# Hybrid streaming encoder on one core: Down's loads and splits issued from a table of steps, and the first FFN unit's token operands made product by product

## The chip, the cores and the metric

The kernel runs on one of the eight cores of a Trainium2 chip. The metric is device time in microseconds (us) of one execution; smaller is better. A core has five engines with queues of their own: PE (TensorE, matrix products), DVE (VectorE), ACT (ScalarE), POOL (GpSimd) and SP, which in this kernel issues nearly all DMA transfers. Each engine runs its queue strictly in order, and semaphores make an instruction wait for another engine or for a transfer.

## The reference

One layer with 1024 prompt tokens and 32 sample tokens (T = 1056), D_MODEL = 1024, D_FF = 2816, all in float32. The change lies in the second half, the ConvFFN:

```python
    x = x + jnp.einsum('ble,ed->bld', jnp.concatenate([y_a, y_b, y_c], axis=-1), w_out)

    h2 = _rmsnorm(x, norm_ffn_g)
    up, gate = jnp.split(jnp.einsum('bld,df->blf', h2, w_up), 2, axis=-1)
    g_conv, new_f = _causal_dwconv(gate, st_f, conv_ffn_w)
    x = x + jnp.einsum('blf,fd->bld', jax.nn.silu(g_conv) * up, w_down)
    return x, (new_a, new_ssm, new_b, new_c, new_f)
```

A final RMSNorm over x gives `y_prompt` and `y_sample`. The mixers ahead of it (short gated conv, Mamba-2 scan, Conformer conv) are not touched.

## The kernel before

**Products in float32 parts.** PE multiplies in the type fp32r. Each operand is split: ACT copies it to fp32r (hi), DVE subtracts that from the original (lo). A product is hi*hi + hi*lo + lo*hi, three matmuls into one PSUM bank. So every operand costs an ACT copy and a DVE subtraction of its size before PE can use it.

**Out-projection, second part (o2).** Its eight products end the first half. After each chunk of tokens (`CH`: 256, 384, 416 columns) `e_o2` writes the new residual row block, adds its square into `ss2`, and scales a copy into `rows[m]`. With the last block (m = 7) `rms_factor` turns `ss2` into `rf`, the reciprocal root, chunk by chunk: a matmul with ones on PE, Sqrt on ACT, RECIPROCAL on DVE (L1007).

**Up.** For each of NF = 22 column blocks f of 128 a `Unit` computes up and gate together by seven Strassen products P1 to P7 over half-sized operands (24 matmuls of 264 columns each). Token operands `X[i, k]` (tiles named XP...: 7 products x 4) are the same for every unit; they are made from `rows` before the first unit: `make_x` forms sums and differences (`xt`), `split_x` the two parts (L1143 on ACT, L1144 on DVE). Weight operands come per unit from `make_sums` (L1162 to L1165) and `make_w` (L1175, L1176), three products ahead. `after` evacuates PSUM: P1's bank is copied to `s1` by ACT (L1292), and P2 accumulates on the same bank, so P2 waits for that copy. `finish` does the causal conv, silu and product, and stores `u` to DRAM (`midd[f]`, L1327).

**Down.** Two passes h over 512 output columns each. In a pass, three groups take the token chunks in the order `CORDER[h]`; in a group PE runs over f: 4 output tiles x 3 matmuls of the chunk's width. Each f needs a weight row block (`next_wd`: load 256 KB, split; kept for the pass) and a token row block (`next_mid`: load, split). Both are iterators, one f per call, called in the loop right ahead of PE's matmuls:

```python
                for f in range(NF):
                    if h == 0 and (n != 1 or f > 14):
                        next_wd()
                    next_mid()
```

Token rows land in `small("midr")`, a ring of 4 buffers; weights land in the pool of 44 shared slots. At f = 21 of Up `next_wd` is called twice and, from the fourth product, `next_mid` twice per product, as a head start. `final` and `final_half` are the closing norms, per chunk, in pass 1.

**What sets the order.** The code is recorded in program order; a scheduler then orders each engine's queue by priority, which is mostly that order, and places waits where a slot is taken over from an earlier user.

Of the kernel before, what the change touches and what calls it, by code (L numbers as in the profile page):

```python
# [9 lines left out]
F32 = mybir.dt.float32  # L10
F32R = mybir.dt.float32r
ALU = mybir.AluOpType
# [4 lines left out]
P = 128  # L17
# [66 lines left out]
def hybrid_stream_encoder_step(  # L84
# [10 lines left out]
    with ctx:  # L95
# [1090 lines left out]
        for m in range(8):  # L1186
# [5 lines left out]
            def e_o2(j, c0, w, ps, m=m, r=r, x=x):  # L1192
# [11 lines left out]
                if j == 2:  # L1204
# [3 lines left out]
                    if m == 6:  # L1208
                        make_w(0, "P1")
                        make_w(0, "P2")  # L1210
                if m == 7:
                    rms_factor(rf, ss2, c0, w, "misc")
                if j == 2:
                    split_x("P2" if m > 3 else "P1", m % 4, x[:, 0:H])

# [2 lines left out]
        for fn in deferred:  # L1218
            fn()
        deferred.clear()  # L1220
        del ss2, rb
        psum.close()
        banks = tc.tile_pool(name="banks", bufs=8, space=PSUM, reuse_waits="tile")
        psum = ExitStack()
# [8 lines left out]
        C2 = [(0, H // 2), (H // 2, H // 2)]  # L1233
        ORDER = ("P1", "P5", "P6", "P2", "P7", "P3", "P4")
        fpack = const.tile([P, 2, 2, NF], F32, name="fpack")
        midd = [dram.tile([P, T], F32, name=f"mid{f}") for f in range(NF)]
        def make_x(i, k):

            a, b = rows[k], rows[k + 4]
# [15 lines left out]
        class Unit:  # L1255
# [62 lines left out]
            def finish(self):  # L1318
                f, gb, u = self.f, self.gb, self.u
                take_state(fpack, gb, 2, f)  # L1320
                ca = slot(T + 2, name="ca")
                for _ in conv_steps(ca, 2, lambda i: pcol(at["w_f"] + NF * i + f), whole(gb, 2)):
                    pass
                act.activation(ca, ca, AF.Silu)
                for t, a, n in run_pieces(2):
                    v.tensor_tensor(out=u[:, t:t + n], in0=ca[:, a:a + n], in1=u[:, t:t + n], op=ALU.mult)
                dma(out=midd[f], in_=u)  # L1327


        wd, mids = {}, {}  # L1330
        w_jobs = iter([(h, f) for h in range(2) for f in range(NF)])
        CORDER = ((0, 1, 2), (2, 1, 0))
        m_jobs = iter([(h, j, f) for h in range(2) for j in CORDER[h] for f in range(NF)])

        def next_wd():
            for h, f in w_jobs:
                r = slot(512, name="rawd")
                dma(out=r, in_=w_down[0, f * P:(f + 1) * P, 512 * h:512 * h + 512])
                w = wd[h, f] = slot(1024, F32R, name="wd")
                act.activation(w[:, 0:512], r, AF.Copy)  # L1340
                v.tensor_tensor(out=w[:, 512:1024], in0=r, in1=w[:, 0:512].bitcast(F32), op=ALU.subtract)
                return

        def next_mid():
            for h, j, f in m_jobs:
                c0, w = CH[j]
                r = small("midr")
                dma(out=r[:, 0:w], in_=midd[f][:, c0:c0 + w])
                q = slot(832, F32R, name="mhl")
                a, b = q[:, 0:416], q[:, 416:832]  # L1350
                act.activation(a[:, 0:w], r[:, 0:w], AF.Copy)  # L1351
                v.tensor_tensor(out=b[:, 0:w], in0=r[:, 0:w], in1=a[:, 0:w].bitcast(F32), op=ALU.subtract)  # L1352
                mids[h, j, f] = (a, b)
                return

        FIRST_ORDER = ("P1", "P2", "P5", "P6", "P3", "P7", "P4")
        for i in FIRST_ORDER[2:]:
            if i == "P5":
                make_sums(0)
            for k in range(4):  # L1360
                make_x(i, k)
            make_w(0, i)
            if i == "P6":
                load_up(1)
        rows.clear()
        xt_.clear()
        steps = [(f, i) for f in range(NF) for i in (ORDER if f else FIRST_ORDER)]
        AHEADW = 3
        for n, (f, i) in enumerate(steps):
            last = f == NF - 1  # L1370
            if n % 7 == 0:
# [3 lines left out]
                make_sums(f + 1)  # L1375
            if 7 <= n + AHEADW < len(steps):
                make_w(*steps[n + AHEADW])
            unit.product(i)
            if n % 7 == 4:
                raws.pop(f)  # L1380
# [2 lines left out]
            if last:  # L1383
                for k in range(4):
                    X.pop((i, k))
                next_wd()
                next_wd()
                if n % 7 > 2:
                    next_mid()
                    next_mid()  # L1390
        del unit, rf
        scope.close()
        scope = ExitStack()

# [65 lines left out]
        for h in range(2):  # L1460
# [4 lines left out]
            for n, j in enumerate(CORDER[h]):  # L1465
# [1 line left out]
                if h and j == 0:  # L1467
                    final_half(0)
                ps = [bank() for _ in range(4)]
                for f in range(NF):  # L1470
                    if h == 0 and (n != 1 or f > 14):
                        next_wd()
                    next_mid()
                    if n == 0 and f in (8, 10, 12, 14):
                        load_res(4 * h + f // 2 - 4)
                    q = wd[h, f]
                    a, b = mids.pop((h, j, f))
                    for m in range(4):
                        o = ps[m][:, 0:w]
                        hi, lo = q[:, m * P:m * P + P], q[:, 512 + m * P:512 + m * P + P]  # L1480
                        pe.matmul(o, hi, a[:, 0:w], start=(f == 0), stop=False)  # L1481
                        pe.matmul(o, hi, b[:, 0:w], start=False, stop=False)  # L1482
                        pe.matmul(o, lo, a[:, 0:w], start=False, stop=(f == NF - 1))  # L1483
                    if n == 2:
                        del wd[h, f], q
                for m in range(4):
                    rc = res[4 * h + m][:, c0:c0 + w]
                    v.tensor_tensor(out=rc, in0=rc, in1=ps[m][:, 0:w], op=ALU.add)
# [35 lines left out]
```

## Time and profile before

| | |
|---|---|
| Time, median of 3 runs | 1572.89 us (1572.78 to 1575.14) |
| The profiled execution's own time | 1571.52 us |
| Its span in the trace | 1569.2 us |
| PE busy | 1497.7 us (95%) |
| DVE busy | 1082.8 us (69%) |
| ACT busy | 606.3 us (39%) |
| Mean granted TensorE clock | 0.983 of full speed |

The time of an execution is 2.3 us more than its span. Busy time is summed over stages with different limits: PE's 95% says that gaps are few, not where they are, and its matmuls are pipelined with modelled ends, so a busy PE can still run at half its clock. What a stage could give back is read from the stage: from the start of its first matmul to that of the next stage's, against the number of matmuls in it and the distance of two matmuls that wait for nothing.

### The profile page before, as it was taken

How to read it: one execution, taken by the hardware profiler on the slowest of the kernel's cores; microseconds unless marked ns; L12 is line 12 of the kernel's file. 1: busy time of each engine (PE TensorE's matmuls, PEld its weight loads, DVE VectorE, ACT ScalarE, POOL GpSimd, SP SyncE). 2: the span in 40 equal slices, each digit the busy share in tenths (PEclk: the TensorE clock that was granted, in tenths of full speed). 3: DMA queues.
4: the chain of work that ended last, by engine and by line, in shares of the span. 5: the costliest groups of instructions: out<-in, count | busy, mean ns of one | idle time of the engine just before them, and what ended most of it. 6: DMA issues, size and time to landing. Idle time of an engine off the chain costs nothing.

```text
span 1569.2 us, 25496 instructions
## 1 busy us (share of the span) xinstructions
PE 1497.7 (95%) x10205; PEld 1455.0 (93%) x10205; DVE 1082.8 (69%) x1677; ACT 606.3 (39%) x1156; POOL 92.2 (6%) x213
## 2 busy tenths in 40 slices
PE   7999999999999899999779999999999977989998
PEld 7999999999989789999779999999999866979998
DVE  7467979598587489675788888888888743343323
ACT  6411112534665374343353333444333333242322
POOL 1000100011121121000020000000000000000000
PEclk9999999999999899999989999999999998999999
DMA  5513011311353586553203322222222256355312
GB/s 189 188 34 102 16 55 45 78 41 41 92 131 97 128 243 165 174 170 126 69 28 89 89 82 82 82 82 82 69 69 69 89 160 201 113 162 176 108 62 101
DMA packets 184420, 163.92 MB, mean 104 GB/s; under 512 B 12117, under 2 KB 165103, under 8 KB 184303
## 3 DMA queue, kind: packets, MB, share of 16 engines
q1 hardware_dynamic: 184287, 162.30, 35.0%
q8 instruction: 80, 1.31, 0.3%
q14 instruction: 37, 0.30, 0.1%
q10 hardware_dynamic: 16, 0.00, 0.0%
HBM read 125.19 MB, written 37.08 MB: 103 GB/s over the span
## 4 chain that ended last, share of the span: by engine, by line
PE 88%; DMA 5%; DVE 4%; ACT 2%; issue 1%; SPq 0%; POOL 0%; ACTq 0%; DVEq 0%; POOLq 0%
PE g L228 14%; PE g L233 14%; PE g L232 13%; PE g L1278 9%; PE g L1280 9%; PE g L1279 9%; PE g L1481 4%; PE g L1482 4%; PE g L1483 4%; DMA rawd<-in_w_down_dram 4%; PE yd L876 1%; PE st L866 1%; PE yo L871 1%; DVE XP L1144 1%; DMA yar<-yad 0%
## 5 line engine op out<-in xcount | busy, mean ns | idle before, releaser
L1278 PE MATMUL g<-XP,wop 128*128 128x264 f32 x1232 | 354.5, 288 | 13.2 <-ACT ps L1292 9.0
L1280 PE MATMUL g<-XP,wop 128*128 128x264 f32 x1232 | 351.7, 286 | 1.4 <-DVE wop L1176 1.4
L1279 PE MATMUL g<-XP,wop 128*128 128x264 f32 x1232 | 352.1, 286 | 0.0
L228 PE MATMUL g<-hH,hi 128*128 128x416 f32 (+2 forms) x952 | 309.7, 325 | 0.0
L232 PE MATMUL g<-hL,hi 128*128 128x416 f32 (+2 forms) x952 | 307.3, 323 | 0.0
L233 PE MATMUL g<-hH,lo 128*128 128x416 f32 (+2 forms) x952 | 307.3, 323 | 0.0
L1278 PEld LDWEIGHTS g<-XP,wop 128*128 128x128 f32 x1232 | 235.3, 191 | 17.9 <-ACT ps L1292 9.2
L1280 PEld LDWEIGHTS g<-XP,wop 128*128 128x128 f32 x1232 | 234.2, 190 | 1.7 <-DVE wop L1176 1.6
L1279 PEld LDWEIGHTS g<-XP,wop 128*128 128x128 f32 x1232 | 234.6, 190 | 0.4 <-issue 0.4
L1481 PE MATMUL g<-mhl,wd 128*128 128x256 f32 (+2 forms) x528 | 159.3, 333 | 26.9 <-ACT mhl L1351 25.3
L228 PEld LDWEIGHTS g<-hH,hi 128*128 128x128 f32 x952 | 179.8, 189 | 1.8 <-issue 1.2
L232 PEld LDWEIGHTS g<-hL,hi 128*128 128x128 f32 x952 | 179.8, 189 | 0.4
L233 PEld LDWEIGHTS g<-hH,lo 128*128 128x128 f32 x952 | 179.6, 189 | 0.5 <-DVE lo L183 0.2
L1482 PE MATMUL g<-mhl,wd 128*128 128x256 f32 (+2 forms) x528 | 175.0, 335 | 2.4 <-DVE mhl L1352 2.2
L1483 PE MATMUL g<-mhl,wd 128*128 128x256 f32 (+2 forms) x528 | 171.5, 328 | 0.0
L273 DVE SCALAR_TENSOR_TENSOR cacc<-cb,par,cacc 128x1086 f32<-128x1086 f32 (+1 forms) x120 | 159.2, 1327 | 7.3 <-ACT cacc L270 5.7
L1352 DVE TENSOR_TENSOR mhl<-midr,mhl 128x256 fp32r<-128x256 f32 (+2 forms) x132 | 67.2, 521 | 89.0 <-ACT mhl L1351 88.5
L1481 PEld LDWEIGHTS g<-mhl,wd 128*128 128x128 f32 x528 | 96.6, 193 | 32.2 <-ACT mhl L1351 29.7
L1482 PEld LDWEIGHTS g<-mhl,wd 128*128 128x128 f32 x528 | 103.0, 195 | 6.9 <-DVE mhl L1352 5.7
L1483 PEld LDWEIGHTS g<-mhl,wd 128*128 128x128 f32 x528 | 103.2, 196 | 0.6
L1351 ACT ACTIVATE mhl<-midr 128x256 fp32r<-128x256 f32 (+2 forms) x132 | 64.0, 493 | 99.6 <-PE g L1483 75.8
L268 ACT ACTIVATE ca<-gb,par 128x1058 f32<-128x1058 f32 x22 | 26.0, 1181 | 185.7 <-issue 159.0
(315 smaller groups left out, 2438.5 us busy)
## 6 DMA issues: line engine op xcount, KB each, us to landing
rawf<-in_w_up_dram SPq DMA_DIRECT2D x44, 512.0 KB
raw<-in_w_in_dram SPq DMA_DIRECT2D x40, 512.0 KB
mid<-u SPq DMA_DIRECT2D x22, 528.0 KB
rawd<-in_w_down_dram SPq DMA_DIRECT2D x44, 256.0 KB
midr<-mid SPq DMA_DIRECT2D x44, 208.0 KB
midr<-mid SPq DMA_DIRECT2D x44, 192.0 KB
E<-acd SPq DMA_DIRECT2D x16, 512.0 KB
midr<-mid SPq DMA_DIRECT2D x44, 128.0 KB
```

The lines of the kernel that those rows point to most:

```text
L228: pe.matmul(o, hi[:, k, :], x, start=first, stop=False)
L232: pe.matmul(o, hi[:, k, :], y, start=False, stop=False)
L233: pe.matmul(o, lo[:, k, :], x, start=False, stop=last)
L273: v.scalar_tensor_tensor(out=out[:, u:u + n], in0=buf[:, b + j:b + j + n], scalar=w_of(j), in1=out[:, u:u + n], op0=ALU.mult, op1=ALU.add)
L1278: pe.matmul(o, hi, xh, start=(new and k == 0), stop=False, **kw)
L1279: pe.matmul(o, hi, xl, start=False, stop=False, **kw)
L1280: pe.matmul(o, lo, xh, start=False, stop=(k == 3), **kw)
L1351: act.activation(a[:, 0:w], r[:, 0:w], AF.Copy)
L1352: v.tensor_tensor(out=b[:, 0:w], in0=r[:, 0:w], in1=a[:, 0:w].bitcast(F32), op=ALU.subtract)
L1481: pe.matmul(o, hi, a[:, 0:w], start=(f == 0), stop=False)
L1482: pe.matmul(o, hi, b[:, 0:w], start=False, stop=False)
L1483: pe.matmul(o, lo, a[:, 0:w], start=False, stop=(f == NF - 1))
```

## The change

**Down.** The two iterators go. A table made beforehand gives each of the 66 steps (a pair of rows f, f + 1 in one group; q counts pairs, NPAIR = 11) the loads and the splits to be issued at it. Loads are of two rows at a time: `[128, 2, 512]` weights, `[128, 2, w]` tokens, for which `midd` becomes 11 DRAM tiles of two rows. Landing tiles all come from the 44 shared slots (`rawd`), token parts too. Token rows are loaded 4 steps and split 2 steps before their use, weights loaded 6 and split 3 steps before in pass 0, and from step 16 on for pass 1. The seven products of the last unit count as steps -7 to -1. Pass 0 takes its chunks widest first, (2, 1, 0) instead of (0, 1, 2).

**First unit.** The token operands of P5, P6, P3, P7 and P4 are no longer all recorded ahead of the unit: `first(i)` is called in the loop, P5's before product 0 (P1), P6's before product 1, and so on (`FIRST_AHEAD`). `rms_factor` for `rf` moves from the end of o2 to behind P4's operands.

```diff
-                if m == 7:
-                    rms_factor(rf, ss2, c0, w, "misc")
...
-        midd = [dram.tile([P, T], F32, name=f"mid{f}") for f in range(NF)]
+        midd = [dram.tile([P, 2, T], F32, name=f"mid{f}") for f in range(NF // 2)]
...
-                dma(out=midd[f], in_=u)
+                dma(out=midd[f // 2][:, f % 2, :], in_=u)
+        NPAIR = NF // 2
+        CORDER = ((2, 1, 0), (2, 1, 0))
+        loads, splits = {}, {}
+        for h in range(2):
+            for q in range(NPAIR):
+                at0 = 3 * NPAIR * h + q
+                c = at0 - 3 if h == 0 else min(at0 - 12, 2 * NPAIR + q - 3)
+                splits.setdefault(c, []).append(("w", h, q))
+                loads.setdefault(c - 3, []).append(("w", h, q))
+            for n, j in enumerate(CORDER[h]):
+                for q in range(NPAIR):
+                    at0 = 3 * NPAIR * h + NPAIR * n + q
+                    splits.setdefault(at0 - 2, []).append(("m", h, q, j))
+                    loads.setdefault(at0 - 4, []).append(("m", h, q, j))
+        rawd, wd, mids = {}, {}, {}
+
+        def prepare(step):
+
+            for job in loads.pop(step, ()):
+                h, q = job[1:3]
+                r = rawd[job] = slot(1024, name="rawd")
+                if job[0] == "w":
+                    src = w_down[0, 2 * q * P:2 * q * P + 2 * P, 512 * h:512 * h + 512]
+                    dma(out=r.rearrange("p (a m) -> p a m", a=2), in_=src.rearrange("(a p) m -> p a m", p=P))
+                else:
+                    c0, w = CH[job[3]]
+                    dma(out=r[:, 0:2 * w].rearrange("p (a w) -> p a w", a=2), in_=midd[q][:, :, c0:c0 + w])
+            for job in splits.pop(step, ()):
+                h, q = job[1:3]
+                r = rawd.pop(job)
+                if job[0] == "w":
+                    for a in range(2):
+                        w = wd[h, 2 * q + a] = slot(1024, F32R, name="wd")
+                        src = r[:, 512 * a:512 * a + 512]
+                        act.activation(w[:, 0:512], src, AF.Copy)
+                        v.tensor_tensor(out=w[:, 512:1024], in0=src, in1=w[:, 0:512].bitcast(F32),
+                                        op=ALU.subtract)
+                else:
+                    w = 2 * CH[job[3]][1]
+                    if w <= 512:
+                        t = slot(1024, F32R, name="mhl")
+                        hi, lo = t[:, 0:w], t[:, 512:512 + w]
+                    else:
+                        hi, lo = slot(w, F32R, name="mh"), slot(w, F32R, name="ml")
+                    act.activation(hi, r[:, 0:w], AF.Copy)
+                    v.tensor_tensor(out=lo, in0=r[:, 0:w], in1=hi.bitcast(F32), op=ALU.subtract)
+                    mids[job[1:]] = (hi, lo)
...
+            if i == "P4":
+                for c0, w in CH:
+                    rms_factor(rf, ss2, c0, w, "misc")
...
+        FIRST_AHEAD = [("P5",), ("P6",), ("P3",), ("P7",), ("P4",), (), ()]
...
+            if f == 0:
+                for i2 in FIRST_AHEAD[n]:
+                    first(i2)
...
-                next_wd()
-                next_wd()
-                if n % 7 > 2:
-                    next_mid()
-                    next_mid()
+                prepare(n % 7 - 7)
...
+                for q in range(NPAIR):
+                    prepare(3 * NPAIR * h + NPAIR * n + q)
```

**Where instructions move: SP's queue at the start of Down.** `rawd<-in_w_down_dram` is a load of weights, `midr<-mid` (before) or `rawd<-mid` (changed) one of token rows, `mid<-u` a unit's store, `res` a residual row. Before, one weight row and one token row in turn:

```order
L1327 DMA mid_7365<-u 128x1056
L1348 DMA midr<-mid_7354 128x256
L1348 DMA midr<-mid_7355 128x256
L1338 DMA rawd<-in_w_down_dram 128x512
L1348 DMA midr<-mid_7356 128x256
L1338 DMA rawd<-in_w_down_dram 128x512
L1348 DMA midr<-mid_7357 128x256
```

Changed, pairs. The rows shown are the last ones ahead of the last unit's store (`mid_7342<-u`):

```order
L1325 DMA mid_7342<-u 128x1056
L1352 DMA rawd<-in_w_down_dram 128x2x512
L1355 DMA rawd<-mid_7332 128x2x416
L1352 DMA rawd<-in_w_down_dram 128x2x512
L1355 DMA rawd<-mid_7333 128x2x416
L1352 DMA rawd<-in_w_down_dram 128x2x512
L1355 DMA rawd<-mid_7334 128x2x416
L474 DMA out_dram<-st_o 44x128 x2
L1352 DMA rawd<-in_w_down_dram 128x2x512
L1355 DMA rawd<-mid_7335 128x2x416
L1352 DMA rawd<-in_w_down_dram 128x2x512
L1355 DMA rawd<-mid_7336 128x2x416
```

Six weight pairs (the first above the rows shown) and five token pairs stand ahead of that store; the sixth token pair and the seventh weight pair stand behind it. There are half as many issues, each of two rows, and no longer one row each of both kinds in turn.

**ACT's queue in the first unit.** The copies L1143 and L1175 are the hi parts (XP50 is P5's first token operand, XP60 P6's, XP30 P3's, XP40 P4's); L1292 (L1290 in the changed kernel) is the copy of P1's bank that P2 waits for. Before, that copy stands behind the hi parts of all operands:

```order
L1143 ACTIVATE XP40_7460<-xt34_7433 128x528
L1143 ACTIVATE XP41_7463<-xt34_7439 128x528
L1143 ACTIVATE XP42_7466<-xt34_7445 128x528
L1143 ACTIVATE XP43_7469<-xt34_7451 128x528
L1175 ACTIVATE wop_7472<-rawf_6890 128x512
L1292 ACTIVATE ps15_7477<-g_7481 128x264
L1292 ACTIVATE ps15_7477<-g_7495 128x264
```

Changed, it stands behind P5's alone; and P5's own copies (`g_7476`, `g_7491`) now stand ahead of P3's operands:

```order
L1143 ACTIVATE XP53_7376<-xt12_7373 128x528
L1175 ACTIVATE wop_7379<-s12_7349 128x512
L1290 ACTIVATE ps15_7345<-g_7382 128x264
L1290 ACTIVATE ps15_7345<-g_7396 128x264
L1143 ACTIVATE XP60_7410<-xt12_7355 128x528
...
L1297 ACTIVATE u_7343<-g_7396 128x264
L1292 ACTIVATE ps15_7345<-g_7476 128x264
L1292 ACTIVATE ps15_7345<-g_7491 128x264
L1143 ACTIVATE XP30_7461<-row4_6898 128x528
```

**DVE's queue.** In the first unit the three reciprocals of `rf`, which before stood among P5's operands and earlier, stand behind P4's operands, ahead of the evacuations of P3 (L1306) and all that follow:

```order
L1144 TENSOR_TENSOR XP43_7573<-xt34_7524,XP43_7573 128x528
L1176 TENSOR_TENSOR wop_7576<-rawf_6890,wop_7576 128x512
L1007 RECIPROCAL rf_6456<-rf_6456 128x256
L1007 RECIPROCAL rf_6456<-rf_6456 128x384
L1007 RECIPROCAL rf_6456<-rf_6456 128x416
L1306 TENSOR_TENSOR u_7343<-g_7476,ps2_7346 128x264
```

At the end of Up (changed), the lo parts of Down's first token pairs (`ml_12745` for step 0, `ml_12796` for step 1) stand between the steps of the last unit's `finish` (`gb`, `ca`):

```order
L1374 TENSOR_TENSOR ml_12745<-rawd_12666,mh_12744 128x832
L1284 TENSOR_TENSOR gb_12531<-g_12605,ps15_12532 128x264
L1284 TENSOR_TENSOR gb_12531<-g_12619,ps15_12532 128x264
L1312 TENSOR_TENSOR gb_12531<-gb_12531,rf_6456 128x528
L273 SCALAR_TENSOR_TENSOR ca_12777<-gb_12531,par_77,ca_12777 128x1058
L1364 TENSOR_TENSOR wd_12789<-rawd_12664,wd_12789 128x512
L273 SCALAR_TENSOR_TENSOR ca_12777<-gb_12531,par_77,ca_12777 128x1058
L1364 TENSOR_TENSOR wd_12792<-rawd_12664,wd_12792 128x512
L1374 TENSOR_TENSOR ml_12796<-rawd_12699,mh_12795 128x832
```

The lo part of step 1's token rows thus follows the last unit's conv and one weight pair's split.

## Rows read from the trace of the kernel before

**Rows 1.** Busy time by stretch (start:end in us, length, then busy us and count of instructions on PE, PE's weight loads, DVE, ACT and POOL, the granted PE clock, the share of the DMA engines and GB/s): the first unit up to P2's resumption, on to the second unit's P7, the 20 units after it, the rest of the last unit, Down's pass 0 by groups (256, 384, 416 columns), pass 1 up to the end.

```profile
769.70:801.40 31.70, 14.26 (x75) 12.97 (x74) 31.46 (x46) 16.07 (x31) 6.46 (x2) 0.74 0.19 54
801.40:827.00 25.60, 25.45 (x193) 25.23 (x193) 21.07 (x40) 11.13 (x22) 4.95 (x5) 0.92 0.17 54
827.00:1239.40 412.40, 411.25 (x3359) 407.79 (x3360) 337.27 (x598) 157.03 (x298) 9.78 (x80) 1.00 0.27 79
1239.40:1252.20 12.80, 10.81 (x75) 10.39 (x74) 8.21 (x16) 6.17 (x13) 1.17 (x2) 0.87 0.42 143
1252.20:1315.00 62.80, 44.36 (x269) 39.50 (x268) 27.54 (x54) 20.87 (x43) 0.00 (x0) 0.88 0.52 168
1315.00:1367.00 52.00, 49.18 (x266) 46.88 (x266) 19.53 (x35) 16.31 (x33) 0.00 (x0) 0.98 0.46 142
1367.00:1423.70 56.70, 50.21 (x262) 48.06 (x261) 25.97 (x47) 22.92 (x43) 0.00 (x0) 1.00 0.57 167
1423.70:1560.00 136.30, 134.71 (x853) 133.21 (x852) 43.41 (x94) 36.29 (x91) 0.00 (x0) 1.00 0.33 103
```

**Rows 2.** Down's matmuls in order of time in three places where none waits (start us, us of one): 384, 416 and 256 columns wide. Six, nine and five intervals lie between the two rows of a pair.

```profile
1349.81 0.33 PE L1481 MATMUL g<-mhl,wd 128*128 128x384 f32 x1
...
1350.86 0.33 PE L1481 MATMUL g<-mhl,wd 128*128 128x384 f32 x1
...
1414.68 0.35 PE L1482 MATMUL g<-mhl,wd 128*128 128x416 f32 x1
...
1416.38 0.35 PE L1482 MATMUL g<-mhl,wd 128*128 128x416 f32 x1
...
1549.80 0.28 PE L1483 MATMUL g<-mhl,wd 128*128 128x256 f32 x1
...
1550.39 0.28 PE L1482 MATMUL g<-mhl,wd 128*128 128x256 f32 x1
```

**Rows 3.** The chain that ended last, in Down's first group, in order of time: start us, length us, what. "SPq" is the issue of a DMA.

```profile
1282.87 0.43 DVE mhl L1352
...
1283.32 0.32 SPq L1348
...
1283.69 2.82 DMA rawd<-in_w_down_dram
...
1286.60 0.64 ACT wd L1340
...
1287.87 0.43 DVE mhl L1352
```

**Rows 4.** Who waited for whom, whole span, SP's queue of DMA issues: total us, times, longest.

```profile
SPq L1327 <- DVE u L1326: 387.6, 22, 24.4
SPq L1348 <- DVE mhl L1352: 159.6, 100, 13.3
```

**Rows 5.** The chain through the units: P7's first matmul in the second unit and in the fifth, three units on.

```profile
827.01 0.39 PE g L1278
...
888.86 0.36 PE g L1278
```

**Rows 6.** PE in order of time at the end of Up (in brackets: idle before, and what ended it) and Down's first matmuls.

```profile
1243.04 0.39 PE L1278 MATMUL g<-XP,wop 128*128 128x264 f32 x1 [0.57 <-ACT wop L1175]
1245.21 0.39 PE L1280 MATMUL g<-XP,wop 128*128 128x264 f32 x1 [1.42 <-DVE wop L1176]
1252.19 0.64 PE L1481 MATMUL g<-mhl,wd 128*128 128x256 f32 x4
```

**Rows 7.** Splits in Down by form: line, engine, operation, tiles and shapes, count, busy us in all, mean ns of one, idle time before them and what ended it.

```profile
L1341 DVE TENSOR_TENSOR wd<-rawd,wd 128x512 fp32r<-128x512 f32 x42 | 29.0, 690 | 61.9 <-ACT wd L1340 61.8
L1340 ACT ACTIVATE wd<-rawd 128x512 fp32r<-128x512 f32 x42 | 26.2, 629 | 81.9 <-DMA rawd<-in_w_down_dram 81.5 <-DVE wd L1341 0.4
L1352 DVE TENSOR_TENSOR mhl<-midr,mhl 128x416 fp32r<-128x416 f32 x36 | 20.9, 589 | 16.6 <-ACT mhl L1351 16.5
L1352 DVE TENSOR_TENSOR mhl<-midr,mhl 128x256 fp32r<-128x256 f32 x22 | 8.9, 417 | 0.0
```

**Rows 8.** ACT and DVE in order of time at the end of a unit: the conv's first tap on ACT, its second on DVE.

```profile
816.70 1.18 ACT L268 ACTIVATE ca<-gb,par 128x1058 f32<-128x1058 f32 x1 [8.29 <-DVE gb L1314]
817.92 1.32 DVE L273 SCALAR_TENSOR_TENSOR ca<-gb,par,ca 128x1058 f32<-128x1058 f32 x1 [1.33 <-ACT ca L268]
```

**Rows 9.** Two stretches of Down's first group (columns as in rows 1).

```profile
1271.00:1292.00 21.00, 16.73 (x108) 14.92 (x108) 9.09 (x19) 7.36 (x17) 0.00 (x0) 0.92 0.55 172
1292.00:1312.00 20.00, 13.67 (x72) 12.05 (x72) 6.14 (x12) 5.56 (x13) 0.00 (x0) 0.83 0.65 220
```

**Rows 10.** DVE in order of time around the first unit: two of the three reciprocals of `rf`.

```profile
763.40 1.75 DVE L1007 RECIPROCAL rf<-rf 128x256 f32<-128x256 f32 x1 [1.30 <-ACT rf L1006]
...
769.84 2.55 DVE L1007 RECIPROCAL rf<-rf 128x384 f32<-128x384 f32 x1
```

**Rows 11.** PE around its waits in the first unit: a matmul of `rms_factor`, P2's first matmul behind its wait, and two of P2's matmuls that wait for nothing.

```profile
775.85 1.75 PE L1005 MATMUL misc<-ss,ones 128*128 128x416 f32 x2 [6.10 <-DVE ss L1203]
...
801.44 0.59 PE L1278 MATMUL g<-XP,wop 128*128 128x264 f32 x1 [9.02 <-ACT ps L1292]
801.83 0.42 PE L1279 MATMUL g<-XP,wop 128*128 128x264 f32 x1
802.04 0.42 PE L1280 MATMUL g<-XP,wop 128*128 128x264 f32 x1
```

More of the change, by code (lines that the diff above doesn't have):

```diff
@@ L1220, in hybrid_stream_encoder_step @@
         deferred.clear()
-        del ss2, rb
+        del rb
         psum.close()
@@ L1326, in finish @@
                     v.tensor_tensor(out=u[:, t:t + n], in0=ca[:, a:a + n], in1=u[:, t:t + n], op=ALU.mult)
-                dma(out=midd[f], in_=u)
[L1330 to L1354, printed above, removed]
+                dma(out=midd[f // 2][:, f % 2, :], in_=u)
@@ L1356, in hybrid_stream_encoder_step, with first @@
         FIRST_ORDER = ("P1", "P2", "P5", "P6", "P3", "P7", "P4")
-        for i in FIRST_ORDER[2:]:
+        def first(i):
             if i == "P5":
@@ L1364, in hybrid_stream_encoder_step @@
                 load_up(1)
-        rows.clear()
-        xt_.clear()
+            if i == "P4":
+                for c0, w in CH:
+                    rms_factor(rf, ss2, c0, w, "misc")
         steps = [(f, i) for f in range(NF) for i in (ORDER if f else FIRST_ORDER)]
         AHEADW = 3
+        FIRST_AHEAD = [("P5",), ("P6",), ("P3",), ("P7",), ("P4",), (), ()]
         for n, (f, i) in enumerate(steps):
@@ L1377, in hybrid_stream_encoder_step @@
                 make_w(*steps[n + AHEADW])
+            if f == 0:
+                for i2 in FIRST_AHEAD[n]:
+                    first(i2)
+                if n == 6:
+                    rows.clear()
+                    xt_.clear()
             unit.product(i)
@@ L1385, in hybrid_stream_encoder_step @@
                     X.pop((i, k))
-                next_wd()
-                next_wd()
-                if n % 7 > 2:
-                    next_mid()
-                    next_mid()
-        del unit, rf
+                prepare(n % 7 - 7)
+        del unit, rf, ss2
         scope.close()
@@ L1469, in hybrid_stream_encoder_step @@
                 ps = [bank() for _ in range(4)]
[L1470 to L1485, printed above, removed]
+                for q in range(NPAIR):
+                    prepare(3 * NPAIR * h + NPAIR * n + q)
+                    if n == 0 and 3 < q < 8:
+                        load_res(4 * h + q - 4)
+                    mh, ml = mids.pop((h, q, j))
+                    for f in (2 * q, 2 * q + 1):
+                        o = f % 2 * w
+                        a, b = mh[:, o:o + w], ml[:, o:o + w]
+                        t = wd[h, f]
+                        for m in range(4):
+                            o = ps[m][:, 0:w]
+                            hi, lo = t[:, m * P:m * P + P], t[:, 512 + m * P:512 + m * P + P]
+                            pe.matmul(o, hi, a, start=(f == 0), stop=False)
+                            pe.matmul(o, hi, b, start=False, stop=False)
+                            pe.matmul(o, lo, a, start=False, stop=(f == NF - 1))
+                        if n == 2:
+                            del wd[h, f], t
                 for m in range(4):
```

## The prediction

> **What bounds the kernel now.** I read four views in this order.
>
> First the busy times by stretch. Of Down's two passes, which do the same matmuls, pass 0 takes 62.8 + 52.0 + 56.7 = 171.5 us and pass 1, closing norms included, 136.3 [rows 1]. PE's granted clock is 0.88 and 0.98 in pass 0's first two groups and 1.00 in the third. Up's 20 middle units run at 1.00 with PE busy throughout. The first unit does not: in its first stretch PE is busy 14.3 of 31.7 us, DVE 31.5.
>
> Second, what pass 0 would take if nothing waited. Two matmuls that wait for nothing start 1.05 / 6 = 0.175 us apart at 384 columns, 1.70 / 9 = 0.189 at 416, 0.59 / 5 = 0.118 at 256 [rows 2]. A group has 22 x 4 x 3 = 264 matmuls: 46.2 + 49.9 + 31.2 = 127.3 us. So pass 0 has an excess of 171.5 - 127.3 = **44.2 us**, of which 62.8 - 31.2 = 31.6 lie in its first group.
>
> Third, whose time that is. The chain repeats a circle about 5.0 us long, 1282.87 to 1287.87: DVE ends a token split, SP may then issue the next token load into the freed buffer, the weight load behind it on the same queue takes 2.8 us, then come ACT's copy, DVE's work, and the next token split [rows 3]. One row takes PE 12 x 0.118 = 1.4 us in that group, so PE follows the circle. Over the span, SP stood 159.6 us, 100 times, at a token load until DVE had split an earlier row [rows 4], and ACT waited 81.5 us for weights to land [rows 7]. That is a serial dependence, not a full DMA: in these stretches the DMA engines are 0.55 to 0.65 busy [rows 9].
>
> Fourth, PE's waits in the first unit: 6.10 us for `rms_factor`'s `ss` and 9.02 for the copy of P1's bank, which stands on ACT behind all token operands [rows 11]. Both times the work that is late is DVE's, or follows DVE's.
>
> **The change part by part.** The sum is made against the profiled execution: span 1569.2, own time 1571.5 (2.3 more), 1.4 below the median of 1572.9.
>
> *End of Up.* A unit takes (888.86 - 827.01) / 3 = 20.62 us [rows 5]; from 827.01, twenty more bring P7 of the last unit to 1239.4. P7, P3 and P4 are 72 matmuls at 20.62 / 168 = 0.123 us: 8.8, end at 1248.2. Before, they end at 1252.2 [rows 6]. The 4.0 lost are two waits for weight operands (0.57 and 1.42) and a clock of 0.87 around them [rows 1, 6]; ACT and DVE came late to those operands because Down's first splits were recorded ahead of them. Now the last products' operands come first. **-4.0.**
>
> *Pass 0.* In the changed order a weight pair is issued 6 steps and a token pair 4 steps before its use; a landing tile is a slot of its own among 44, and the waits on slots that the order shows go to users that end several steps earlier. With the circle gone, what must keep up per step? In the widest group, which comes first, a step is 24 x 0.189 = 4.5 us of PE. DVE has two weight splits at 0.69 and one token split of 832 columns: by (589 - 417) / 160 = 1.07 ns per column beyond 416, 1.03 us; 2.4 in all [rows 7]. ACT has two copies at 0.63 and one below that of DVE, 2.3 at most. DMA has 512 + 416 KB, 0.95 MB, in 4.5 us: 209 GB/s. The DMA engines moved 220 at a share of 0.65 [rows 9], which scales to 338. In the 256-column group a step is 2.84 us with 256 KB of tokens; pass 1's weights begin 17 steps ahead of use: for five steps 786 KB per 2.84 us, 277 GB/s, 0.82 of the scaled rate. I take it that none of these is late: **-44.2.** Issuing two rows at once also halves what each load adds in overhead; I price that at nothing, since with 4 steps (18 us) of lead a load of 2.8 us is hidden behind PE's matmuls. If that cover is gone, the circle is back (rivals).
>
> *Down's first two steps.* This is new. Step 1's lo part stands on DVE behind the last unit's conv. Let T0 be the end of P4. DVE finishes step 0's lo part at about T0 + 0.8, evacuates and scales the gate by T0 + 2.1; ACT's first tap takes 1.18, DVE's two taps 1.32 each [rows 8], the two weight splits between them 0.69 each, the lo part 1.03: T0 + 8.3. PE has the first four matmuls of step 0 (0.75), four transposes of `fpack` (0.6), the other 20 (3.8), and four that need only the hi part of step 1 (0.75): T0 + 5.9. It stands 2.4 us. After waits of this size PE runs on slowly for a while: P2's matmuls stood 0.21 us apart, against 0.123, behind their wait [rows 11], and the pass's clock of 0.83 to 0.92 is that of stretches with such waits [rows 9]. I put that at 1.5, between nothing and the whole of a step at half clock, 4.5. Sum 2.4 + 1.5 + 0.6 = **+4.5**; bounds 0.6 (the finish overlaps better) and 9.
>
> The last unit's store is a second place. It waits for DVE's product `u` (T0 + 9.3), and on SP's queue the sixth token pair and the seventh weight pair are behind it. SP stood 387.6 us for those stores in 22 units [rows 4]; what is queued behind waits too. The pair is issued at about T0 + 10, lands by T0 + 13, and is split long before step 5, T0 + 25: nothing. The Trainium skill's page "DMA: Bandwidth & Descriptors", section "Anatomy of one DMA", says that any semaphore wait happens on the issuing sequencer before dispatch; the trace agrees (387.6 us), and it is the rule that speaks against this change, since the schedule's lead ends at a queue that stands. By it a store 15 us later than I reckon would bring the wait back to PE.
>
> *First unit.* Here I expect nearly nothing. From 769.7 to 827.0 DVE is busy 31.46 + 21.07 = 52.5 of 57.3 us [rows 1], and P7 at 827.0 follows DVE. The change takes no DVE work out; it reorders it. It brings one piece in: the 256-column reciprocal, 1.75 us, ran ahead of the stretch in DVE's idle time [rows 10]. So DVE has 54.3 us here. PE's waits of 6.1 and 9.0 us leave their places, but DVE sets when P5, P6 and P3 can run, so PE waits there instead, a product at a time, at half clock (0.21 between matmuls, [rows 11]). New idle time on DVE: P3's operands stand on ACT behind P5's evacuations, which wait for PE's slow P5, about 3.2; and P4's end to the conv, 1.8 to 4.2. Together 5.0 to 7.4, where it was 4.8. The stretch starts 1.1 earlier without `rms_factor`'s matmuls in o2. The marker: 769.7 - 1.1 + 54.3 + 5.0 to 7.4 = 827.9 to 830.3; with PE some 11 matmuls (1.3 us) further along when it gets there, -0.4 to +2.0. I take **+1.0**, bounds -5 (all of DVE's idle time goes) and +4.
>
> Sum: -4.0 - 44.2 + 4.5 + 1.0 = -42.7. Span 1526.5, own time 1528.8, median **1530.2**; I say 1530.
>
> **The rivals.**
>
> *Down is still limited by its loads, in part.* In one stretch of 21 us the engines moved only 172 GB/s [rows 9]. At that rate a widest step takes 0.95 / 0.172 = 5.5 us, 1.0 more than PE's, 11 times: +11, 1541; with the 256-column group's five heavy steps late too (786 KB at 172 is 4.6 us, +1.7 each), 1549. For it: 220 is the highest rate those stretches show, and 338 is only scaled. Against: the engines were idle a third of the time then, waiting for issues.
>
> *The first unit gives its waits back.* If DVE's idle time there vanishes, -5 in place of +1: 1524. Against: the sum of DVE's work, 54.3 us. For: PE's 9.0 us wait is real and its cause, the copy's place, is removed.
>
> *Nothing gained.* The table does not take effect because slots come free as late as `midr` did: 1573. The order speaks against it.
>
> *Slower.* If each of pass 0's 33 steps waits for a slot that PE frees only in the step before, then issue 0.3, load 2.8 to 3.4, ACT 0.6 and DVE 1.0 stand in PE's path: about 5 us x 33 = 165, less the 44.2 that I count as gained. It decides at 44.2 / 33 = 1.3 us per step. In the order the slots are released 2 steps or more ahead, so I hold it unlikely.
>
> A page's reckoning of load size, in a sentence by itself: the Trainium skill's "SBUF — State Buffer" fits a transfer at 2 us + bytes / 436 GB/s, which would put 512 KB at 3.2 us and 256 KB at 2.6 (an estimate); the trace has 2.8 for the 256 KB, and the sum does not use it.
>
> **How the numbers follow.** Forecast as summed, 0.73 (own range 1524 to 1536, from Down's start at 0.6 to 9 and the first unit at -0.4 to +2); loads in part 0.13 (1537 to 1569); first unit gives back 0.09 (1520 to 1525); nothing 0.02; slower 0.03. About 0.2%, 3 us, is what a measurement here can tell from no change. Faster: 0.73 + 0.13 + 0.09 = 0.95; within 0.2%: 0.02; slower 0.03. The range 1521 to 1541 leaves out most of the slow half and the last of the fast end.
>
> **What would show it.** Right: pass 0 at 130 to 134 us and clock near 1.00 from its third step; SP's waits for DVE's token splits gone; one wait of PE for `ml` in step 1; the second unit's P7 near 828; DVE busy without gaps there but at P3's operands. Wrong: PE waits for `mh` or `wd` after step 3, or ACT for `rawd`, would show loads that limit; P7 of the second unit below 824 would show that the first unit was not DVE's; a wait in step 5 would be the store's.

## The result and the profile after

The changed kernel takes **1531.38 us** (median; 1530.48 to 1532.33), the kernel before 1573.56 in the same comparison: ratio 0.9731, interval 0.9714 to 0.9748. The forecast was 1530, range 1521 to 1541. The profiled execution's span is 1528.4 us, 40.8 less than before; the forecast for the span was 1526.5.

Where it went, from the starts of matmuls in the two traces (us). The first row is the start of o2's first product, work that the change does not touch; in the fourteen traces here that start lies between 674.06 and 680.38, whatever the edit, so its +1.2 is scatter:

| stage | before | after | difference | forecast |
|---|---|---|---|---|
| start to o2's products | 674.06 | 675.28 | +1.2 | 0 |
| o2 and first units, up to P7 of the fifth unit | 214.80 | 217.76 | **+3.0** | +1.0 |
| on to P7 of the last unit | 350.55 | 350.70 | +0.2 | 0 |
| last unit's P7, P3, P4 | 12.79 | 8.70 | **-4.1** | -4.0 |
| Down, pass 0 | 171.93 | 130.69 | **-41.2** | -39.7 |
| pass 1 to the end | 145.08 | 145.30 | +0.2 | 0 |

The busy times of the changed kernel by stretch, columns as in [rows 1]: first unit up to the sums before the second unit's P7, the rest of the last unit, pass 0 by groups (416, 384, 256 columns):

```profile
769.80:830.70 60.90, 42.62 (x279) 40.23 (x278) 54.00 (x85) 29.09 (x55) 0.96 (x4) 0.83 0.19 56
...
1243.40:1252.40 9.00, 9.00 (x77) 9.00 (x76) 5.82 (x12) 3.37 (x6) 1.29 (x2) 1.00 0.84 311
1252.40:1305.70 53.30, 50.84 (x269) 49.34 (x268) 34.23 (x46) 26.49 (x39) 0.00 (x0) 1.00 0.68 242
1305.70:1351.50 45.80, 45.80 (x266) 45.80 (x265) 13.48 (x20) 9.62 (x15) 0.00 (x0) 1.00 0.41 127
1351.50:1383.10 31.60, 31.60 (x265) 31.60 (x264) 20.47 (x30) 17.94 (x28) 0.00 (x0) 1.00 0.76 232
```

The 384 and 256 groups take about what 264 unhindered matmuls take (46.2 and 31.2 from [rows 2]), with PE busy throughout. The widest group is 3.4 over its 49.9. The granted clock is 1.00 from the last unit on; before, it was 0.87 to 0.98 in the last unit and in pass 0's first two groups [rows 1].

Who waited in pass 0 of the changed kernel (us, times, longest): first all of PE's waits, then some of SP's, then ACT's for landed token rows.

```profile
PE g L1511 <- DVE ml L1374: 1.9, 1, 1.9
PE g L1510 <- ACT mh L1373: 0.5, 1, 0.5
```

```profile
SPq L1355 <- PE g L1512: 43.6, 13, 8.3
...
SPq L1355 <- DVE ml L1374: 8.4, 2, 4.5
...
SPq L1355 <- DVE mhl L1374: 7.5, 5, 1.7
SPq L1325 <- DVE u L1324: 5.3, 1, 5.3
```

```profile
ACT mh L1373 <- DMA rawd<-mid: 9.2, 7, 3.0
```

SP still stands for slots, 43.6 us in 13 waits of its token loads for PE, but PE does not wait for what is behind. Two of the forecast's signs came out otherwise: SP's waits for token splits are not gone (15.9 us in 7 waits), and ACT did wait for `rawd` (9.2 us), a sign named for loads that limit. Neither reached PE after step 1. The last unit's store (L1325) held the queue 5.3 us and reached nothing. PE's two waits are both in step 1, in order of time:

```profile
1258.19 1.02 PE L1510 MATMUL g<-mh,wd 128*128 128x416 f32 x4 [0.48 <-ACT mh L1373]
1261.10 0.46 PE L1511 MATMUL g<-ml,wd 128*128 128x416 f32 x1 [1.89 <-DVE ml L1374]
1261.39 0.35 PE L1512 MATMUL g<-mh,wd 128*128 128x416 f32 x1
1261.58 0.35 PE L1511 MATMUL g<-ml,wd 128*128 128x416 f32 x1
```

The step waits 2.37 us in all; from the second matmul behind the wait they are 0.19 apart again, the unhindered distance.

In the first unit, PE's long waits, then DVE's one long idle stretch and the start of the reciprocals:

```profile
779.84 0.86 PE L1276 MATMUL g<-XP,wop 128*128 128x264 f32 x2 [7.16 <-ACT wop L1175]
801.40 0.59 PE L1276 MATMUL g<-XP,wop 128*128 128x264 f32 x1 [5.21 <-ACT wop L1175]
813.57 0.56 PE L1276 MATMUL g<-XP,wop 128*128 128x264 f32 x1 [3.04 <-DVE u L1306]
```

```profile
789.61 0.71 DVE L1144 TENSOR_TENSOR XP<-row,XP 128x528 fp32r<-128x528 f32 x1 [3.73 <-ACT XP L1143]
...
806.36 6.78 DVE L1007 RECIPROCAL rf<-rf 128x256 f32<-128x256 f32 x3
```

PE's waits of 6.10 and 9.02 us [rows 11] have become waits of 7.16, 5.21 and 3.04 at other products; with the shorter ones, PE waits 18.3 us there against 17.5 before. P7 of the fifth unit, at 888.86 before [rows 5], comes 4.2 us later, 1.2 of it from the later start:

```profile
893.04 0.36 PE L1276 MATMUL g<-XP,wop 128*128 128x264 f32 x1
```

### The profile page after: what moved, and what is told of

The parts are those of the page before. It is cut to its first block, busy times and chain, and to the rows that moved or that the text cites. A ratio compares the mean times of both kernels' runs of the same rounds, so it can differ in the third digit from the quotient of the medians.

```text
span 1528.4 us, 25030 instructions
## 1 busy us (share of the span) xinstructions
PE 1481.9 (97%) x10205; PEld 1447.3 (95%) x10205; DVE 1073.4 (70%) x1611; ACT 594.4 (39%) x1090; POOL 84.5 (6%) x213
## 3 DMA queue, kind: packets, MB, share of 16 engines
q8 instruction: 80, 1.31, 0.4%
## 4 chain that ended last, share of the span: by engine, by line
PE 91%; DVE 4%; DMA 2%; ACT 1%; issue 1%; SPq 0%; POOL 0%; ACTq 0%; DVEq 0%
PE g L228 14%; PE g L233 13%; PE g L232 13%; PE g L1276 10%; PE g L1278 9%; PE g L1277 9%; PE g L1511 5%; PE g L1512 5%; PE g L1510 5%; DMA yar<-yad 1%; PE yd L876 1%; PE st L866 1%; PE yo L871 1%; DMA zr<-zd 1%; DVE XP L1144 1%
## 5 line engine op out<-in xcount | busy, mean ns | idle before, releaser
L1276 PE MATMUL g<-XP,wop 128*128 128x264 f32 x1232 | 354.7, 288 | 18.1 <-ACT wop L1175 13.6
L273 DVE SCALAR_TENSOR_TENSOR cacc<-cb,par,cacc 128x1086 f32<-128x1086 f32 (+1 forms) x120 | 159.6, 1330 | 7.3 <-ACT cacc L270 5.7
L1511 PE MATMUL g<-ml,wd 128*128 128x384 f32 (+1 forms) x352 | 120.7, 343 | 2.0 <-DVE ml L1374 1.9
L1510 PE MATMUL g<-mh,wd 128*128 128x384 f32 (+1 forms) x352 | 119.5, 343 | 2.3 <-DVE y L1451 1.8
L1512 PE MATMUL g<-mh,wd 128*128 128x384 f32 (+1 forms) x352 | 120.3, 342 | 0.0
L1374 DVE TENSOR_TENSOR ml<-rawd,mh 128x832 fp32r<-128x832 f32 (+1 forms) x44 | 43.4, 990 | 83.9 <-ACT mh L1373 53.6
L183 DVE TENSOR_TENSOR lo<-raw,hi 128x1024 fp32r<-128x1024 f32 x56 | 68.9, 1231 | 21.9 <-ACT hi L188 21.8
L273 DVE SCALAR_TENSOR_TENSOR ca<-gb,par,ca 128x1058 f32<-128x1058 f32 x44 | 58.1, 1319 | 28.7 <-ACT ca L268 28.7
L1373 ACT ACTIVATE mh<-rawd 128x832 fp32r<-128x832 f32 (+1 forms) x44 | 38.1, 871 | 96.1 <-PE g L1511 53.3
L1510 PEld LDWEIGHTS g<-mh,wd 128*128 128x128 f32 x352 | 65.9, 188 | 3.2 <-ACT y L1443 2.1
```

What stands on the lines that cost most here:

```text
L183: v.tensor_tensor(out=lo, in0=r, in1=hi.bitcast(F32), op=ALU.subtract)
L273: v.scalar_tensor_tensor(out=out[:, u:u + n], in0=buf[:, b + j:b + j + n], scalar=w_of(j), in1=out[:, u:u + n], op0=ALU.mult, op1=ALU.add)
L1276: pe.matmul(o, hi, xh, start=(new and k == 0), stop=False, **kw)
L1374: v.tensor_tensor(out=lo, in0=r[:, 0:w], in1=hi.bitcast(F32), op=ALU.subtract)
L1510: pe.matmul(o, hi, a, start=(f == 0), stop=False)
L1511: pe.matmul(o, hi, b, start=False, stop=False)
```

## The experiments

Each kernel is compared with the kernel before, run on the same chip (1574 to 1575 us in these comparisons). "Pass 0" and other stages are again differences of matmul starts in its trace.

**Down alone, first unit alone.** `e1`: the changed kernel with `rms_factor` back in o2 and `FIRST_AHEAD` empty, `first(i)` called for all products ahead of the loop. `e2`: the kernel before with `FIRST_AHEAD` and the moved `rms_factor`.

> Down's table, with the first unit as before (all token operands recorded ahead of it, rms_factor at the end of o2). Theory (the first unit's part costs about 2.8 us, all of it on DVE, and Down's part alone gives 43 to 44): 1528.6 us, P7 of the second unit near 827 plus whatever the run starts late, pass 0 at 130 to 132. Rival (the later P7 in the changed kernel is only its later start, and the first unit's part costs nothing): 1531 us.

Measured: 1527.71 us, ratio 0.9702 (0.9686 to 0.9719). Pass 0 130.7; up to the fifth unit's P7 214.5, as before.

> The first unit's part alone, Down as before. Theory: 2.8 us slower than before, 1576.4 us; DVE idle 3 to 4 us at P3's first operand, PE's two long waits moved to P5 and P3 and not removed. Rival (it gives PE's 9 us wait back and the loss in the changed kernel is due to something else): 1568 to 1573 us.

Measured: 1578.74 us, ratio 1.0026 (1.0016 to 1.0035), up to the fifth unit's P7 217.8 (before 214.8), and DVE's idle 3.75 us at P3's first operand as in the changed kernel. The two parts add up: 1574.16 - 46.45 + 4.58 = 1532.3, against 1531.4. All of the gain is Down's; the first unit's part costs. Its cost is nearer to the 3.0 us of its own stage: in the trace of `e2` pass 0, whose code is as before, is also 3.2 longer (175.1), and whether that is scatter is not shown.

**What in Down's old order was the bound.** First the ring of landing tiles, twice; `e3` takes a shared slot in its place, `e10` a pool of 8 of its own:

```diff
-                r = small("midr")
+                r = slot(416, name="midr")                                        # e3
+                r = rings[0].tile([P, 416], F32, tag="mr", name="midr") if rings else small("midr")  # e10
```

> Before, with one line changed: a token row lands in one of the 44 shared slots in place of the ring of 4. One row per load, old order, no table. Theory (the ring of 4 closes the circle of load, copy, split, and is the cause of most of the excess of pass 0): pass 0 at 145 us or less, time 1547 or less. Rival (the cause is that loads and splits are recorded one row ahead of their use, so a larger ring changes little): pass 0 above 160, time above 1562.

Measured: 1571.25 us, ratio 0.9979 (0.9968 to 0.9991). Pass 0 162.8, and pass 1 to the end 154.4 in place of 145.1. By these numbers the rival's expectation is met. But that a larger ring "changes little" does not hold where the circle was: the first group is 48.9 in place of 62.5, and the third is longer, 63.7 in place of 57.5. In pass 1 ACT waits 69.7 us for token rows to land, 13.1 before; that the shared slots which token rows took are the reason is not shown. Two effects are mixed; hence the next run.

> Before, with the ring for token rows twice as large (8 in a pool of their own, so that the shared slots are not touched) and nothing else. Theory of the prediction (the ring of 4 closes the circle): pass 0 145 us or less, time under 1550. Theory after the run with shared slots (the ring is about a third of it, in the first group alone): pass 0 157 to 163, 1560 to 1566 us, pass 1 as before. Rival (the ring is nothing): 1572 to 1575 us.

Measured: 1575.53 us, ratio 1.0009 (0.9998 to 1.0020), pass 0 175.8. Doubling the ring gives nothing. The chain in its first group, and then SP's waits for token splits in the first group: of the kernel before, of `e10`, and of `e3`.

```profile
1277.97 0.35 DVE mhl L1352
1278.33 0.33 SPq L1348
1278.71 2.59 DMA rawd<-in_w_down_dram
1281.32 0.64 ACT wd L1340
1281.99 0.69 DVE wd L1341
1282.68 0.35 DVE mhl L1352
```

```profile
SPq L1348 <- DVE mhl L1352: 47.6, 15, 13.3
SPq L1348 <- DVE mhl L1352: 46.7, 12, 14.0
SPq L1348 <- DVE mhl L1352: 1.0, 3, 0.4
```

It is the circle of [rows 3] again, 4.7 us long. With twice the ring, the scheduler moves each token load four rows further ahead in SP's queue; it still waits for a token split, and the weight load behind it is the same one, needed two rows later. With the 44 slots of `e3` that wait is gone, and the first group is 13.6 us shorter, though SP stands there for a state output (14.9 us) and for the last unit's store (9.1) instead. So the circle has two links that could be opened: the token load's wait, which 8 buffers do not end and the shared slots do, and the place of the weight load behind it. If the second is a link, the circle should open when the weight load alone is moved:

```diff
+        def load_wd(n):
+            while len(raw_q) < n:
...
         def next_wd():
             for h, f in w_jobs:
-                r = slot(512, name="rawd")
-                dma(out=r, in_=w_down[0, f * P:(f + 1) * P, 512 * h:512 * h + 512])
+                load_wd(7 if h == 0 else 1)
+                r = raw_q.pop(0)
```

> Before, with one part changed: in pass 0 each weight row's load is recorded 6 rows ahead of its split (before: right ahead of it). Ring of 4, single rows, group order and splits as before. Theory (what closes the circle is not the size of the ring but that a weight load stands on SP behind a token load that waits for a split, two rows ahead of its own split, which in turn stands on ACT and DVE ahead of the next token split): the first group falls from 62.5 to 42 us or less, pass 0 to 150 or less, 1553 us or less. Rival (the loads cannot come faster in the narrow group, or the ring holds the token rows): first group 55 or more, 1565 us or more.

Measured: **1540.84 us**, ratio 0.9779 (0.9763 to 0.9795), with the ring of 4, single rows and the old group order. Its pass 0 by groups (256, 384, 416 columns), PE's waits there, and SP's waits for token splits, over the span and in the first group:

```profile
1252.00:1285.70 33.70, 31.99 (x268) 31.31 (x267) 24.77 (x46) 17.96 (x38) 0.00 (x0) 1.00 0.77 244
1285.70:1336.80 51.10, 48.15 (x265) 45.83 (x266) 19.35 (x37) 16.16 (x32) 0.00 (x0) 1.00 0.47 139
1336.80:1394.40 57.60, 50.91 (x265) 48.73 (x264) 26.34 (x47) 22.49 (x43) 0.00 (x0) 1.00 0.56 168
```

```profile
PE g L1494 <- ACT mhl L1364: 10.4, 8, 2.2
```

```profile
SPq L1361 <- DVE mhl L1365: 127.0, 93, 3.2
SPq L1361 <- DVE mhl L1365: 11.9, 11, 3.2
```

The first group fell from 62.5 to 33.7 (31.2 if nothing waited), at 1.00 of the clock. The last unit's closing products fell from 12.8 to 9.4. SP's waits for token splits fell by 32.6 us, from 159.6 [rows 4] to 127.0, and nearly all of that is in and just ahead of the first group: 47.6 to 11.9 (13.3 of the 47.6 are one wait that began before Down). The 112.0 us behind the first group stayed (111.9). What is left, 4.9 and 7.7 us in the other two groups, is token rows that come late (PE waits for `mhl`). This one edit gives 34.0 us of the 46.5 that Down's table gives alone (`e1`). It does two things that no run separates: the weight loads leave the circle, and 18 of them are issued before Down's first matmul, 9 before the edit. Which part of the table gives the other 12.5 is argued from these waits, the earlier token rows, and shown by no run of its own.

**The other parts of the schedule.** `e11` is the kernel before with `CORDER = ((2, 1, 0), (2, 1, 0))`; the next three are the changed kernel with one thing undone: `e7` `CORDER = ((0, 1, 2), (2, 1, 0))`; `e8` two loads of one row in place of each pair; `e9` `at0 - 1` and `at0 - 2` for token splits and loads.

> Before, with one line changed: pass 0 takes its groups widest first, (2, 1, 0). Ring of 4, one row per load, iterators as they were. Theory (the group that loads weights and tokens together is the one that lacks time; at 416 columns a row gives 2.27 us of PE to hide them, at 256 columns 1.42): pass 0 140 to 150 us, 1543 to 1553 us. Rival (the circle takes its time whatever the width): pass 0 above 165, 1566 us or more.

Measured: 1562.00 us, ratio 0.9919 (0.9904 to 0.9934), pass 0 159.9, first group 67.0. Between the two: 3.05 us per row is more than the 2.84 that a row took with 256 columns first, so the circle does not take its time whatever the width, yet more of it is covered by PE.

> The changed kernel with pass 0's groups in the old order, 256 columns first. Theory (the order of the groups matters: with 256 columns first the weights of the pass, 512 KB, and 256 KB of tokens are wanted every 2.84 us for 11 steps, 277 GB/s, more than the 220 to 250 seen in any stretch so far): pass 0 5 to 15 us longer, 1537 to 1546 us, first group 36 to 46 us in place of 31.2. Rival (only the lead and the landing tiles matter, and the DMA engines could move 338): 1531 to 1533 us.

Measured: 1533.00 us, ratio 0.9734 (0.9718 to 0.9751): pass 0 133.1, 2.4 longer. The first group lies within the theory's 36 to 46 us, but the pass and the time do not; the theory falls, and the rival's 1533 is met. The first group:

```profile
1251.30:1289.00 37.70, 33.99 (x269) 33.40 (x268) 26.73 (x43) 23.02 (x38) 0.00 (x0) 0.95 0.84 295
```

37.7 us, 6.5 over. 3.7 of it are two waits in the first steps, 1.60 and 2.10, behind which 13 matmuls ran 0.21 apart in place of 0.12. And 295 GB/s was moved where I had seen no more than 250:

```profile
1256.33 0.74 PE L1510 MATMUL g<-mhl,wd 128*128 128x256 f32 x4 [1.60 <-ACT mhl L1373]
1259.17 0.58 PE L1511 MATMUL g<-mhl,wd 128*128 128x256 f32 x1 [2.10 <-DVE mhl L1374]
```

> The changed kernel with each load of two rows issued as two loads of one row; table, tiles and splits unchanged. Theory (priced at nothing: four steps of lead hide it): 1530 to 1533 us. Rival (half as many loads is what relieves SP's queue): 5 us slower or more, with waits of ACT for rawd in Down.

Measured: 1529.92 us, ratio 0.9717 (0.9701 to 0.9733); pass 0 130.6. Pairing is worth nothing that shows, as priced.

> The changed kernel with token rows loaded 2 steps and split 1 step before their use, in place of 4 and 2. Theory (once landing tiles are not in the way, two steps of 4.5 or 2.8 us hide a load of about 3 us and the splits): 1531 to 1536 us, PE's waits in Down under 5 us more. Rival (it is the long lead that removes the excess): 10 to 30 us slower, with waits of PE for mh or ml in most steps of pass 0.

Measured: 1540.43 us, ratio 0.9782 (0.9766 to 0.9798). Pass 0 is 131.7, so two steps of lead are enough in the steady state; the rival falls. The theory is off too: 4.5 us are lost ahead of Down and 3.5 in pass 1. The first is one wait:

```profile
1257.79 1.76 PE L1510 MATMUL g<-mh,wd 128*128 128x416 f32 x4 [4.36 <-ACT mh L1373]
```

The copy of step 0's token rows then stands on ACT behind the last unit's conv tap:

```profile
1254.73 1.18 ACT L268 ACTIVATE ca<-gb,par 128x1058 f32<-128x1058 f32 x1 [7.50 <-DVE gb L1312]
1255.82 1.13 ACT L1363 ACTIVATE wd<-rawd 128x512 fp32r<-128x512 f32 x2
1256.86 0.88 ACT L1373 ACTIVATE mh<-rawd 128x832 fp32r<-128x832 f32 x1
```

The lead matters at the edges of a stage, where other work stands in the queues.

**The first unit, and step 1.** `e5`: P3's operands recorded together with P6's. `e15`: this, `rms_factor` back in o2, and the token rows of the first four steps one step earlier. `e16`: `e1` with this last edit.

```diff
-        FIRST_AHEAD = [("P5",), ("P6",), ("P3",), ("P7",), ("P4",), (), ()]
+        FIRST_AHEAD = [("P5",), ("P6", "P3"), (), ("P7",), ("P4",), (), ()]       # e5, e15
...
-                    splits.setdefault(at0 - 2, []).append(("m", h, q, j))
-                    loads.setdefault(at0 - 4, []).append(("m", h, q, j))
+                    splits.setdefault(at0 - (3 if at0 < 4 else 2), []).append(("m", h, q, j))   # e15, e16
+                    loads.setdefault(at0 - (5 if at0 < 4 else 4), []).append(("m", h, q, j))
```

> The changed kernel with P3's token operands recorded one product earlier, together with P6's, so that their copies stand ahead of P5's evacuations on ACT. Theory (DVE sets the second unit's P7, and its idle 3.7 us at P3's first operand is part of the 4 us that the first unit lost): 2 to 4 us faster than the changed kernel, 1527 to 1529 us. Rival (PE's slow stretch sets it, DVE's idle time only moves): 1530 to 1533 us.

Measured: 1528.17 us, ratio 0.9701 (0.9687 to 0.9715). DVE's idle 3.7 us is gone, and the stretch to the fifth unit's P7 is 214.2, 3.6 less than in the changed kernel: DVE sets it.

> Down's table with the first unit as before (1527.7 us measured) and the token rows of Down's first four steps loaded and split one step earlier. Theory: step 1's waits of 0.5 and 1.9 us and the slow matmuls behind them go, 2.5 to 4 us faster, 1523.5 to 1525.5 us. Rival (the same work then stands ahead of the last unit's conv and makes its store late, so that a later step waits): 1527 us or more.

Measured: 1524.52 us, ratio 0.9683 (0.9663 to 0.9703), pass 0 127.5.

> The changed kernel with three edits: P3's operands one product earlier, rms_factor back at the end of o2, and the token rows of Down's first four steps loaded and split one step earlier. Theory: the first 3, the second 1.5 (one reciprocal of 1.75 us out of DVE's busy stretch), the third 2.5 to 4 us (the wait of 1.9 us in step 1 and the slow matmuls behind it): 1522 to 1525 us. Rival (the first unit's time is PE's, and what is taken from step 1 goes to the last unit's finish): 1528 us or more.

Measured: **1521.89 us**, ratio 0.9662 (0.9648 to 0.9675), the fastest of all and 0.1 below the theory's range. Its pass 0 by groups, and PE's longest waits in the first unit:

```profile
1247.40:1297.40 50.00, 50.00 (x268) 49.42 (x267) 34.33 (x46) 25.71 (x38) 0.00 (x0) 1.00 0.67 247
1297.40:1343.20 45.80, 45.80 (x266) 45.80 (x265) 13.46 (x20) 9.63 (x14) 0.00 (x0) 1.00 0.43 127
1343.20:1374.90 31.70, 31.70 (x267) 31.70 (x266) 21.07 (x31) 18.15 (x29) 0.00 (x0) 1.00 0.74 234
```

```profile
785.06 0.44 PE L1278 MATMUL g<-XP,wop 128*128 128x264 f32 x1 [2.39 <-ACT wop L1175]
802.81 0.59 PE L1278 MATMUL g<-XP,wop 128*128 128x264 f32 x1 [4.33 <-ACT wop L1175]
```

Pass 0 is now the 127.3 of unhindered matmuls. In the first unit PE's 9 us wait is gone, and still only 1.1 us against the kernel before came of it (213.7 against 214.8 up to the fifth unit's P7): DVE's sum of work stands.

## Why the prediction was right, and where it was not

**The bound.** Right in place: the excess of pass 0 over 127.3 us was recoverable, and the circle of [rows 3] is what held most of it. Nothing in the argument showed *which* link to open, and it named "the freed buffer". The runs show two links. Twice as many buffers opened nothing (`e10`, 1575.5), because the token loads moved ahead by as much and SP's wait stayed; enough of them ended the wait and took 13.6 us off the first group (`e3`), at a loss elsewhere. The weight load's place behind the waiting token load, with too short a lead over its own split, was worth 28.8 us there (`e14`, 1540.8; place and lead are moved together). SP's 159.6 us [rows 4] were a sum over stages with different prices: the 47.6 in the first group fell to 11.9 in `e14`, and the 112.0 behind it stayed and had little price. The Trainium skill's page "DMA: Bandwidth & Descriptors", section "Anatomy of one DMA", has the wait on the issuing sequencer ahead of dispatch; the traces of `e10` and `e14` agree (46.7 and 11.9 us in the first group), and show what it means here: a load pays for the wait of the load ahead of it.

**End of Up, -4.0.** Measured -4.1, with a reason that was half right. The forecast blamed the place of Down's first splits ahead of the last unit's operands. `e14` leaves them recorded there and has only its weight loads earlier, and the stage falls from 12.8 to 9.4: most of the loss was splits that stood for their load. In the kernel before, ACT with an operand of the last unit (`wop`) behind such a split:

```profile
1241.24 1.23 ACT L1340 ACTIVATE wd<-rawd 128x512 fp32r<-128x512 f32 x2 [5.18 <-DMA rawd<-in_w_down_dram]
1242.37 0.61 ACT L1175 ACTIVATE wop<-s 128x512 fp32r<-128x512 f32 x1
```

**Pass 0, -44.2:** the last two groups reached their bound, and `e15` reached it in all three.

**Down's first two steps, +4.5.** Measured 3.4 (130.7 against 127.3). The wait was forecast at 2.4 and is 2.37, the transposes at 0.6; the term that was too large is the slow running behind the wait, put at 1.5. About 0.4 is left for it. It had been taken from P2's matmuls behind a 9 us wait; behind 1.89 us PE was back at its full distance within two matmuls (in `e7`, behind two waits in a row, it was not: 13 slow ones, 1.2 us).

**The store.** It held SP for 5.3 us, and no step waited: as forecast.

**First unit, +1.0.** Measured +3.0, above the likeliest case's upper end. The sum of DVE's work was right, 54.0 of the 60.9 us in the first row of the changed kernel's stretches against 54.3, and its idle time of 6.9 lies inside 5.0 to 7.4. At the sums ahead of the second unit's P7 (L1165) DVE is 4.0 us later than before (829.31 against 825.33), 2.8 without the later start, where the middle of the forecast was 2.1. The step that failed is the last: "with PE some 11 matmuls (1.3 us) further along". PE's waits came back as 5.21 and 3.04 us, and inside P7 as 0.42, 0.85 and 1.31. At the last of them PE was 7 matmuls further than at 827.01 before, and the next dozen stood 0.22 apart in place of 0.12, so that nothing was left of the lead:

```profile
830.66 0.59 PE L1278 MATMUL g<-XP,wop 128*128 128x264 f32 x1 [1.31 <-DVE wop L1176]
831.04 0.42 PE L1276 MATMUL g<-XP,wop 128*128 128x264 f32 x1
831.26 0.42 PE L1277 MATMUL g<-XP,wop 128*128 128x264 f32 x1
```

The matmul at 827.01 in [rows 5] is P7's second; its first starts at 826.60, and at 827.00 in the changed kernel. The loss thus comes within P7, which this marker of the forecast could not show.

**The rivals.** Loads that limit: `e7` moved 295 GB/s in its group, and the changed kernel 409 for 13 us (last section), so 172 was the circle's rate, not the engines', and the scaled 338 was too low a bound. The first unit giving its waits back: fell, by the sum of DVE's work. Slower, by a slot wait in each step: SP's 13 waits for PE exist, none reached PE.

The result, 1531.4, lies 1.4 above the forecast, and the span 1.9 above its own: first unit +2.0 and the later start +1.2, which is scatter, are offset by Down's -1.5; the rest is small. That the numbers met so closely is in part luck, two errors of opposite sign.

## What to carry to other kernels

When a chain shows load, split, load in a circle, ask of each link what stands ahead of it in its queue, before asking for more buffers: moving one load a few rows up gave 34 us here, doubling the ring of the load ahead of it gave nothing. Read the waits of an issuing queue by stage: of SP's 159.6 us the 47.6 in one group went with nearly all of that gain, and 112.0 stayed. Reordering operands ahead of a stage gave next to nothing here while the engine that makes them was busy throughout; look at that engine's own idle time instead.

## What was not expected

The DMA engines moved far more than the stretches of Down before had shown, 172 and 220 GB/s in [rows 9]. In the changed kernel, with loads of 512, 416 and 384 KB and residual rows queued one behind the other, they held 409 GB/s for 13 us (columns as in [rows 1]; packets count where they start, so that the share can pass 1):

```profile
1268.00:1281.00 13.00, 13.00 (x70) 12.89 (x70) 11.39 (x16) 8.71 (x13) 0.00 (x0) 1.00 1.05 409
```

The row that gives this away was in the kernel before, far from Down, among its first transfers:

```profile
46.00:50.20 4.20, 4.20 (x27) 3.33 (x26) 2.10 (x4) 2.09 (x4) 0.00 (x0) 1.00 1.03 417
```

A rate scaled from a stretch that waits for issues, 338 in the prediction, is not the engines' limit; a busier stretch of the same trace shows more.
